# Gate and up products of a hybrid encoder layer by seven block products in place of eight

## The chip, the cores and the metric

The kernel runs on one core of a Trainium2 chip. The metric is the device time of one execution in microseconds; lower is better. The kernel before was timed three times: 723.5, 723.86 and 723.93 us, median 723.86 us.

## The reference, cut to what matters

One layer of an encoder trunk over 512 tokens with 1024 features, all in float32: latent attention and a gated linear recurrence side by side, an output projection, a gated feed-forward part and a per-layer embedding gate. The change lies in the feed-forward part, whose inner width D_FF is 2816, that is 22 tiles of 128 columns.

```
a = mla(c_q, c_kv, k_r, ...)
r = hgrn2(hq, hf_f, hf_b, hi, hg, ...)
x = x + concatenate([a, r]) @ w_o
h = rms_norm(x, g_ffn)
x = x + (silu(h @ w_gate) * (h @ w_up)) @ w_down
gate = sigmoid(rms_norm(x, g_ple) @ w_ple_gate)
x = x + gate * (p @ w_ple_proj)
```

## The kernel before, in words

Activations lie with features on partitions: x is eight tiles `xT[k]` of 128 features by 512 tokens. TensorE multiplies in float32r, so every operand is split into a high part (ScalarE copies it to float32r) and a low part (VectorE subtracts the high part from the operand); `split` does this. A product is then three matmuls, high by high, high by low and low by high (`mm3`, lines 137 to 139), all added up in one PSUM bank. Weights come by DMA from the SyncE queue in chunks of 128 by up to 1024 (`weights`, line 143): a `raw` tile from a pool of four, a `whi` and a `wlo` tile from pools of WB = 3 each. All other tiles of 128 by 512 come from 74 slots that the program hands out itself (`Slots`), the one that has been free longest first; PSUM's eight banks are handed out in the same way.

Up to about 300 us two streams run side by side, the input projections with the recurrence and the attention. Then the second half of the output projection (`w_o_half(1, ...)`) makes the last sums of x, four tiles at a time: k outside, the four output tiles inside. `residual` adds each to x, scales it with the norm's gains and splits it (`hh`, `hl`, lines 133 and 134), and adds its squares for the norm. The factor 1/rms by token (`token_rstd`) isn't multiplied into h: it is put on the products when they leave PSUM (`bc2`).

The feed-forward part (line 947 on) goes through the 22 tiles of the inner width in three parts of 8, 7 and 7 (FPARTS). For each tile f it loads the chunk of `w_gate` and then that of `w_up` (128 by 1024: eight k blocks of 128), multiplies each with all eight feature tiles (eight k, 24 matmuls of 512 columns into a bank `ff`), multiplies with `bc2` on the way out (line 957), applies Silu to the gate, multiplies both (line 962) and splits the result (`ah`, `al`). At the end of a part come the down products: for each of eight output tiles m one chunk of `w_down` and nf x 3 matmuls into a bank `dn`, added to x by `residual`. After the three parts follow the gate of the per-layer embeddings (`pg`) and the output.

The program is written in order and without semaphores. A planner in the tile framework lays out the order of the instructions on each engine: it runs through the program with a cost for each instruction, and each engine takes what is ready, first in program order. So an instruction can be drawn forward past one that isn't ready by the planner's reckoning. On the chip each engine keeps the order laid out and waits where something isn't there. A tile from a pool is given to the instruction that writes it first, once all users of an earlier one have been through.

Of the kernel before, what the change touches and what calls it, by code (L numbers as in the profile page):

```python
# [8 lines left out]
F32 = mybir.dt.float32  # L9
# [6 lines left out]
P = 128  # L16
S = 512
# [5 lines left out]
FPARTS = (8, 7, 7)  # L23
SLOTS = 74
# shares of the two streams
L_TOTAL, D_TOTAL = 97, 135
AHEAD = 2
WB = 3
# [8 lines left out]
# columns of the packed per-partition vectors  # L37
V_MIX, V_FFN, V_PLE, V_QA, V_KVA, V_QN, V_KN, V_LB, V_HGO = 0, 8, 16, 24, 26, 28, 29, 30, 46
NV = 50
# columns of the packed rows (the same for every partition)  # L40
R_QN, R_KN = 0, 64
NR = 128
# columns of the constants that depend on shapes alone
# [11 lines left out]
class Slots:  # L55
    """Tiles of one size, handed out by hand: the one that has been free longest comes next."""
# [19 lines left out]
    def part(self, prefix, n):  # L76
        """Slots of their own from the free ones."""
        s = Slots(self.pool, 0, self.prefix)
        s.free.extend(self.free.popleft() for _ in range(n))
        s.count = 1000 * ord(prefix)  # L80
        return s
# [7 lines left out]
def merge(streams):  # L89
    """Runs generators side by side, by the shares of their totals that they have yielded. One that  # L90
    yields a condition waits until it holds."""
# [16 lines left out]
def v3(t, a, b=None):  # L108
    """A tile's 512 columns as (a, b)."""
    return t.rearrange("p (a b) -> p a b", a=a)  # L110
# [3 lines left out]
def layer_kernel(ctx: ExitStack, tc: tile.TileContext, io, out):  # L114
# [11 lines left out]
    # ---------------------------------------------------------------- helpers  # L126
    def split(hi, lo, src, scale=None, eng=dve):
        """src (times a scale per partition) = hi + lo, each exact in float32r."""
# [14 lines left out]
    def weights(src, cols, lo_eng=None):  # L143
        """A chunk of weights [128, cols]: its parts hi and lo."""
# [13 lines left out]

    def rsqrt_mean(o, ss, n):
        """o = (ss / n + eps) ** -0.5, for a few columns."""  # L160
        w = ss.shape[-1]
        v = small.tile([P, 8], F32, tag="rs_v", name="rs_v")
        dve.tensor_scalar(v[:, :w], ss, 1.0 / n, EPS, ALU.mult, ALU.add)  # L163
        pool.tensor_tensor(o, v[:, :w], mhalf[:, :w], ALU.pow)  # L164

    def token_rstd(sq, keep=None):
        """From sums of squares [128 of the features, tokens]: 1/rms by token, tokens on
        partitions [128, 4] and on columns, the same on every partition [128, 512]."""
# [6 lines left out]
        # the diagonal matrices of 1 / rms, summed over the partitions  # L175
# [13 lines left out]
    def squares(acc, src, first):  # L189
        """acc += src ** 2"""  # L190
# [8 lines left out]
    # ---------------------------------------------------------------- inputs  # L199
# [11 lines left out]
    # loads the activation engine's table while the first inputs are under way  # L211
    act.activation(small.tile([P, 1], F32, tag="first", name="first"), mhalf[:, :1], AF.Exp)

    # ---------------------------------------------------------------- input projection, latents
    # the query's latents, features on partitions
    hT = [(A.get(f"hh{k}", F32R), A.get(f"hl{k}", F32R)) for k in range(KT)]
    cq = [B.get(f"cq{m}") for m in range(2)]
    # the tensor engine's clock rises while it is busy
# [31 lines left out]
    # those of key and value and the rotary key, tokens on partitions  # L250
# [23 lines left out]
    # ---------------------------------------------------------------- rotary tables  # L274
# [17 lines left out]
    # cos(r) = sin(pi / 2 - |r|)  # L292
# [9 lines left out]
    def rope(eng, o, x, c, s, t1, t2):  # L302
        """o = x * [cos, cos] + [x2, x1] * [-sin, sin], all [128, a, 64]"""
# [5 lines left out]
    # ---------------------------------------------------------------- lower bounds of the gates  # L309
# [14 lines left out]
    # ================================================================ latent attention  # L324
# [4 lines left out]
    def attention():  # L329
        """Emits the attention in pieces; yields the tensor engine's time for each."""  # L330
        # 1 / rms of the latents, with the one of the input
        sc = cpool.tile([P, 2 * NT], F32, name="sc")  # by token: query, key and value
# [28 lines left out]
        # the shared rotary key, with its gains, turned  # L361
# [8 lines left out]
        def wsmall(name, cols):  # L370
            """A small matrix of two chunks, two halves each."""
# [11 lines left out]
        # keys and values; per head, tokens on partitions: [128, tile, 128]  # L383
# [3 lines left out]
        rt = [A.get(f"rk{j}") for j in range(NT)]  # rotary parts by tile: [128, (key, query) x head, 64]  # L387
# [67 lines left out]
        def features(tok, g):  # L455
            """[128 tokens, tile, 128] to [128 features, tokens], times gains: hi and lo."""
# [9 lines left out]
        def rotary(pr):  # L466
            """Of two heads: the key's parts (hi, hi) and (lo, lo), the query's (hi, lo)."""
# [78 lines left out]
    # ================================================================ HGRN2  # L546
    # 1 at every step but a chunk's first, for the sums along the chunks
# [7 lines left out]
    # chunks of weights for the dense stream, one ahead of its use  # L555
# [11 lines left out]
    def w_in_tile(d):  # L567
        """One tile of 128 of the input projection's columns: [128 columns, tokens]"""
# [11 lines left out]
    def w_in_tokens(evacuate):  # L580
        """512 columns of the input projection, tokens on partitions, 256 at a time."""
# [16 lines left out]
    def gates(heads):  # L598
        """q, and for each direction k and the sums of log f along the chunks."""
# [10 lines left out]
        # one table of the activation engine after the other  # L610
# [13 lines left out]
        for (h, d), f in zs.items():  # L624
            # log f = log max(f, c) + log min(f / c, 1)
# [17 lines left out]
    def together(emit):  # L643
        """The first, whose operand comes last, and the others right behind it."""
# [5 lines left out]
    def output_gates():  # L650
        """Features on partitions, with the gains of the output norm."""
# [19 lines left out]
    def decays(h):  # L671
        """Of one head, both directions: queries and keys with the decays that go with them."""
        yield lambda: ("gates", h) in done
        for d in range(2):
# [7 lines left out]
            # exponentials of the sums: to the chunk's middle, from there to its end, to its end  # L682
# [17 lines left out]
            # the same for tiles of two chunks  # L700
# [16 lines left out]
    def within(h):  # L717
        """What reaches a step from its own tile of two chunks, as weights [128 s, tile, 128 t]."""
        pd = BL.get("pd")  # within chunks: [128 (chunk, s), direction, tile, 64 t]
        pd4 = pd.rearrange("p (d j t) -> p d j t", d=2, j=NT)  # L720
        px = BL.get("px")  # from a tile's earlier chunk to its later one
# [27 lines left out]
    def carried(h):  # L749
        """The states before the tiles, both directions."""  # L750
# [50 lines left out]
    def finish(h):  # L801
        """Norm, gate and layout of one head's outputs."""
# [27 lines left out]
    def w_o_half(half, src, banks):  # L830
        """x += (src as rows of features) @ half of the output projection's rows"""
        for c in range(2):
            ws = [wnext() for _ in range(2)] if half else None
            os_ = []
            for m in range(4 * c, 4 * c + 4):
# [12 lines left out]
            if half:  # L848
# [4 lines left out]
                for i in range(4):  # L853
                    residual(4 * c + i, os_[i], V_FFN, sq2, h2)
                banks.put(*os_)

# [62 lines left out]
    wlist.extend((io["w_or"][c], 1024) for c in range(4))  # L919
# [4 lines left out]
    def residual(m, o, g, sqacc, hs):  # L924
        """x[m] += o; its squares and its parts hi and lo, with the next norm's gains."""
        dve.tensor_tensor(xT[m], xT[m], o, ALU.add)  # L926
        if g is not None:
            hl = (A.get("hh", F32R), A.get("hl", F32R))
            split(hl[0], hl[1], xT[m], vec[:, g + m : g + m + 1])
            hs.append(hl)  # L930
            squares(sqacc, xT[m], m == 0)

    B = BD.join(BL)
    sq2 = A.get("sq2")
    h2 = []
# [7 lines left out]
    # ---------------------------------------------------------------- feed-forward  # L943
# [3 lines left out]
    for part, nf in enumerate(FPARTS):  # L947
        acts = []
        for f in range(f0, f0 + nf):
            zz = []  # L950
            for name in ("w_gate", "w_up"):
                w = weights(io[name][f], 1024)
                o = B.get("ff")
                for k in range(KT):
# [124 lines left out]
```

## Time and profile before

| what | number |
|---|---|
| runs | 723.5, 723.86, 723.93 us |
| span of the profiled execution | 721.8 us |
| TensorE (matmul) busy | 703.6 us, 97% |
| VectorE busy | 439.3 us, 61% |
| ScalarE busy | 309.2 us, 43% |
| GpSimd busy | 135.8 us, 19% |
| read from memory | 63.68 MB |

The profiled execution has only its span (first to last instruction); the timed runs lie 1.7 to 2.1 us above it, for what comes before and after. Line numbers (L137) are those of the kernel before. Names are those of the program without their numbers: `ff<-hh,whi` is a matmul into a gate or up bank from a feature tile and a weight tile. A matmul's listed duration runs from its start to its result, and neighbours overlap.

### The profile page before, as it was taken

The numbers are of one execution on the slowest core, as the hardware profiler recorded it, in microseconds if no ns is written. First come the engines' busy times: TensorE is split into PE (matmuls) and PEld (weight loads), VectorE is DVE, ScalarE is ACT, GpSimd is POOL, SyncE is SP. The second block draws the span as 40 slices with busy tenths as digits, with TensorE's granted clock in tenths as the row PEclk, the third lists the DMA queues.
The fourth block names the chain that finished last, engine by engine and source line by source line (L and its number), as shares of the span: only waits on it lengthen the run. The fifth ranks groups of instructions, "written<-read, shape, count | busy, mean of one in ns | idle before, by whom it ended". The sixth has DMA issues, their size and how long they took to land.

```text
span 721.8 us, 9167 instructions
## 1 busy us (share of the span) xinstructions
PE 703.6 (97%) x3516; PEld 588.5 (82%) x3516; DVE 439.3 (61%) x733; ACT 309.2 (43%) x573; POOL 135.8 (19%) x126
## 2 busy tenths in 40 slices
PE   8999997998999999999999999999999999999997
PEld 6888885897878888788888888888888888888886
DVE  8954469988999984386545334435433444456573
ACT  5566785576554635355233222223222223244341
POOL 7983577010543511001000000000000000000000
PEclk9999999999999999999999999999999999999999
DMA  8432112111034221033232322232233232233211
GB/s 282 167 114 93 59 36 81 59 30 60 15 103 156 60 78 59 30 118 116 96 109 87 104 101 87 91 114 77 79 108 117 90 108 87 78 105 116 89 59 58
DMA packets 22075, 66.36 MB, mean 92 GB/s; under 512 B 2704, under 2 KB 3984, under 8 KB 22032
## 3 DMA queue, kind: packets, MB, share of 16 engines
q1 hardware_dynamic: 22032, 65.79, 28.0%
q8 instruction: 27, 0.44, 0.2%
q14 instruction: 16, 0.13, 0.1%
HBM read 63.68 MB, written 2.10 MB: 91 GB/s over the span
## 4 chain that ended last, share of the span: by engine, by line
PE 85%; DVE 8%; ACT 3%; DMA 2%; issue 1%; SPq 1%; POOL 0%; ACTq 0%; POOLq 0%
PE ff L137 11%; PE ff L138 11%; PE ff L139 11%; PE dn L138 6%; PE dn L137 6%; PE dn L139 6%; PE wi L139 3%; PE wi L137 3%; PE wi L138 3%; PE pg L139 2%; PE pg L138 2%; PE pg L137 2%; PE wo L137 2%; PE wo L139 2%; PE wo L138 2%; PE po L787 1%
## 5 line engine op out<-in xcount | busy, mean ns | idle before, releaser
L130 ACT ACTIVATE whi<-raw 128x1024 fp32r<-128x1024 f32 (+4 forms) x114 | 116.2, 1019 | 286.6 <-issue 103.1
L131 DVE TENSOR_TENSOR wlo<-raw,whi 128x1024 fp32r<-128x1024 f32 (+4 forms) x108 | 133.7, 1240 | 26.1 <-ACT whi L130 24.8
L137 PE MATMUL ff<-hh,whi 128*128 128x512 f32 x352 | 137.0, 390 | 0.1
L138 PE MATMUL ff<-hl,whi 128*128 128x512 f32 x352 | 136.8, 389 | 0.0
L139 PE MATMUL ff<-hh,wlo 128*128 128x512 f32 x352 | 136.8, 389 | 0.0
L957 DVE TENSOR_TENSOR z<-ff,rsbc 128x512 f32<-128x512 f32 x44 | 30.1, 691 | 109.8 <-PE ff L139 109.2
L164 POOL TENSOR_TENSOR rs_tok<-rs_v,mhalf 128x4 f32<-128x4 f32 x3 | 4.7, 1568 | 391.7 <-DVE rs_v L163 391.7
L137 PEld LDWEIGHTS ff<-hh,whi 128*128 128x128 f32 x352 | 66.1, 188 | 14.3 <-ACT whi L130 0.5
L138 PEld LDWEIGHTS ff<-hl,whi 128*128 128x128 f32 x352 | 66.1, 188 | 13.7
L139 PEld LDWEIGHTS ff<-hh,wlo 128*128 128x128 f32 x352 | 66.1, 188 | 13.6
L137 PE MATMUL dn<-ah,whi 128*128 128x512 f32 x176 | 68.5, 389 | 0.0
L138 PE MATMUL dn<-al,whi 128*128 128x512 f32 x176 | 68.5, 389 | 0.0
L139 PE MATMUL dn<-ah,wlo 128*128 128x512 f32 x176 | 68.5, 389 | 0.0
L139 PE MATMUL wi<-hh,wlo 128*128 128x512 f32 x128 | 51.7, 404 | 3.6 <-DVE wlo L131 3.6
L926 DVE TENSOR_TENSOR x<-x,dn 128x512 f32<-128x512 f32 x24 | 16.5, 687 | 60.5 <-PE dn L139 60.5
L138 PE MATMUL wi<-hl,whi 128*128 128x512 f32 x128 | 51.4, 401 | 0.0
L137 PE MATMUL wi<-hh,whi 128*128 128x512 f32 x128 | 51.0, 400 | 0.0
L137 PEld LDWEIGHTS dn<-ah,whi 128*128 128x128 f32 x176 | 33.0, 188 | 6.9
L139 PEld LDWEIGHTS dn<-ah,wlo 128*128 128x128 f32 x176 | 33.0, 188 | 6.8
L138 PEld LDWEIGHTS dn<-al,whi 128*128 128x128 f32 x176 | 33.0, 188 | 6.8
L139 PEld LDWEIGHTS wi<-hh,wlo 128*128 128x128 f32 x128 | 24.5, 191 | 8.9 <-DVE wlo L131 4.0
L138 PEld LDWEIGHTS wi<-hl,whi 128*128 128x128 f32 x128 | 24.4, 191 | 4.9
(287 smaller groups left out, 1361.9 us busy)
## 6 DMA issues: line engine op xcount, KB each, us to landing
raw<-in_w_gate SPq DMA_DIRECT2D x22, 512.0 KB, 3.3
raw<-in_w_up SPq DMA_DIRECT2D x22, 512.0 KB, 3.2
raw<-in_w_hf SPq DMA_DIRECT2D x16, 512.0 KB, 3.7
raw<-in_w_d SPq DMA_DIRECT2D x16, 448.0 KB, 3.2
x<-in_xT SPq DMA_DIRECT2D x16, 256.0 KB, 5.2
raw<-in_w_d SPq DMA_DIRECT2D x8, 512.0 KB, 3.3
raw<-in_w_pg SPq DMA_DIRECT2D x8, 512.0 KB, 3.2
raw<-in_w_i SPq DMA_DIRECT2D x4, 512.0 KB, 3.4
```

The lines of the kernel that those rows point to most:

```text
L130: act.activation(hi, src, AF.Copy)
L131: eng.tensor_tensor(lo, src, hi, ALU.subtract)
L137: pe.matmul(o, lhsT=l[0], rhs=r[0], start=start, stop=False)
L138: pe.matmul(o, lhsT=l[0], rhs=r[1], start=False, stop=False)
L139: pe.matmul(o, lhsT=l[1], rhs=r[0], start=False, stop=stop)
L164: pool.tensor_tensor(o, v[:, :w], mhalf[:, :w], ALU.pow)
L787: pe.matmul(po[:, ts(j)], lhsT=l, rhs=r, start=n == 0, stop=n == len(terms) - 1)
L926: dve.tensor_tensor(xT[m], xT[m], o, ALU.add)
L957: dve.tensor_tensor(z, o, bc2, ALU.mult)
```

## The change

Two weight tiles f and f + 1 (256 columns of the inner width) are multiplied together. The rows are cut in k 0 to 3 and k 4 to 7, so each matrix is two by two blocks: A11 and A12 are the chunk of f, A21 and A22 that of f + 1; the features are cut in the same two halves of k and in two halves of 256 tokens, B11, B12, B21, B22. The product of two by two blocks takes seven block products instead of eight, by the scheme with sums S1 to S4 of weight blocks, T1 to T4 of feature blocks, and sums of the results. A block product is four k by three matmuls of 256 columns.

`weight_blocks` loads both chunks and makes the four sums of weights on GpSimd, 128 by 512 each; `feature_blocks` makes those of the features on GpSimd once, 128 by 256 each, and `split_blocks` splits them. `products` runs the seven products in three PSUM banks and the sums of results on VectorE. The last sum, S4, of gate and up shares one tile for both (`last_sums`). WB goes from 3 to 4, the pool `sums` has three tiles, the slots go from 74 to 68, and FPARTS from (8, 7, 7) to (8, 8, 6), for even parts; the second half of the output projection makes the x tiles in pairs k and k + 4.

```diff
-FPARTS = (8, 7, 7)
-SLOTS = 74
+FPARTS = (8, 8, 6)
+SLOTS = 68
-WB = 3
+WB = 4
+HS = S // 2
...
+    def weight_blocks(src1, src2, u, last):
+        nw[0] += 1
+        r1 = wpool.tile([P, 1024], F32, tag="raw", bufs=RAWB, name=f"raw{nw[0]}a")
+        r2 = wpool.tile([P, 1024], F32, tag="raw", bufs=RAWB, name=f"raw{nw[0]}b")
+        u1 = wpool.tile([P, 1024], F32, tag="sums", bufs=3, name=f"sums{nw[0]}")
+        sp.dma_start(r1, src1)
+        sp.dma_start(r2, src2)
+        a11, a12, a21, a22 = r1[:, :512], r1[:, 512:], r2[:, :512], r2[:, 512:]
+        s1, s2 = u1[:, :512], u1[:, 512:]
+        t, thi, tlo = u
+        s4 = slice(last * 512, last * 512 + 512)
+        pool.tensor_tensor(s1, a21, a22, ALU.add)
+        pool.tensor_tensor(a21, a11, a21, ALU.subtract)
+        pool.tensor_tensor(s2, s1, a11, ALU.subtract)
+        pool.tensor_tensor(t[:, s4], a12, s2, ALU.subtract)
+        out = {}
+        for n, src, names in (("1", r1, ("A11", "A12")), ("2", r2, ("S3", "A22")), ("3", u1, ("S1", "S2"))):
+            hi = wpool.tile([P, 1024], F32R, tag="whi", name=f"whi{nw[0]}{n}")
+            lo = wpool.tile([P, 1024], F32R, tag="wlo", name=f"wlo{nw[0]}{n}")
+            split(hi, lo, src)
+            for i, name in enumerate(names):
+                out[name] = cut((hi, lo), i * 512, i * 512 + 512)
+        split(thi[:, s4], tlo[:, s4], t[:, s4])
+        out["S4"] = thi[:, s4], tlo[:, s4]
+        return out
+    def last_sums():
+        nw[0] += 1
+        return (wpool.tile([P, 1024], F32, tag="sums", bufs=3, name=f"sums{nw[0]}"),
+                wpool.tile([P, 1024], F32R, tag="whi", name=f"whi{nw[0]}"),
+                wpool.tile([P, 1024], F32R, tag="wlo", name=f"wlo{nw[0]}"))
+    def feature_blocks(z1, z2, t3):
+        c = A.get("t24")
+        pool.tensor_tensor(t3, z2[:, HS:], z1[:, HS:], ALU.subtract)
+        pool.tensor_tensor(z1[:, HS:], z1[:, HS:], z1[:, :HS], ALU.subtract)
+        pool.tensor_tensor(c[:, :HS], z2[:, HS:], z1[:, HS:], ALU.subtract)
+        pool.tensor_tensor(c[:, HS:], z2[:, :HS], c[:, :HS], ALU.subtract)
+        return c
+    def split_blocks(blocks, z1, z2, c):
+        for src, names in ((z1, ("B11", "T1")), (z2, ("B21", "B22")), (c, ("T2", "T4"))):
+            hl = (A.get("bh", F32R), A.get("bl", F32R))
+            split(*hl, src)
+            A.put(src)
+            blocks["tiles"].append(hl)
+            for i, name in enumerate(names):
+                blocks[name].append(cut(hl, i * HS, i * HS + HS))
+    def products(w, b, bank):
+        n = len(b["B11"])
+        def product(o, left, right, start):
+            for k in range(n):
+                l, r = cut(w[left], k * P, k * P + P), b[right][k]
+                kw = dict(skip_group_check=not start)
+                pe.matmul(o, lhsT=l[0], rhs=r[0], start=start and k == 0, stop=False, **kw)
+                pe.matmul(o, lhsT=l[0], rhs=r[1], start=False, stop=False, **kw)
+                pe.matmul(o, lhsT=l[1], rhs=r[0], start=False, stop=k == n - 1, **kw)
+        o1, o2, o3 = (bank.get(f"st{i}") for i in range(3))
+        product(o1[:, :HS], "S2", "T2", True)
+        product(o1[:, HS:], "A11", "B11", True)
+        product(o2[:, :HS], "S3", "T3", True)
+        qc = A.get("qc")
+        act.copy(qc[:, HS:], o1[:, HS:])
+        dve.tensor_tensor(qc[:, :HS], o1[:, :HS], qc[:, HS:], ALU.add)
+        product(o3[:, :HS], "S1", "T1", True)
+        dve.tensor_tensor(qc[:, HS:], o2[:, :HS], qc[:, :HS], ALU.add)
+        product(o1[:, HS:], "A12", "B21", False)
+        z1, z2 = A.get("z1"), A.get("z2")
+        dve.tensor_tensor(z2[:, HS:], o3[:, :HS], qc[:, HS:], ALU.add)
+        product(o2[:, :HS], "A22", "T4", False)
+        product(o3[:, :HS], "S4", "B22", False)
+        return z1, z2, qc, (o1, o2, o3)
...
+            ms = (2 * c, 2 * c + 1, 2 * c + 4, 2 * c + 5) if half else range(4 * c, 4 * c + 4)
+            for m in ms:
                 if not half and m % 2 == 0:
                     w = wnext()
                 o = banks.get("wo")
@@ -850,9 +942,10 @@
                     for i in range(4):
                         a = ((i % 2) * 4 + k) * P
                         mm3(os_[i], cut(ws[i // 2], a, a + P), src[k], k == 0, k == 3)
-                for i in range(4):
-                    residual(4 * c + i, os_[i], V_FFN, sq2, h2)
+                for i in (0, 2, 1, 3):
+                    residual(ms[i], os_[i], V_FFN, sq2, h2)
                 banks.put(*os_)
+                ffn_blocks(c)
...
-    wlist.extend((io["w_or"][c], 1024) for c in range(4))
+    wlist.extend((io["w_or"][c], 1024) for c in (0, 2, 1, 3))
...
-            hl = (A.get("hh", F32R), A.get("hl", F32R))
-            split(hl[0], hl[1], xT[m], vec[:, g + m : g + m + 1])
-            hs.append(hl)
+            if g == V_FFN:
+                hs[m] = A.get("xg")
+                act.activation(hs[m], xT[m], AF.Copy, scale=vec[:, g + m : g + m + 1])
+            else:
+                hl = (A.get("hh", F32R), A.get("hl", F32R))
+                split(hl[0], hl[1], xT[m], vec[:, g + m : g + m + 1])
+                hs.append(hl)
             squares(sqacc, xT[m], m == 0)
+    hb = {n: [] for n in ("B11", "B21", "B22", "T1", "T2", "T3", "T4", "tiles")}
+    def ffn_blocks(c):
+        d = A.get("t3")
+        for i in range(2):
+            k = 2 * c + i
+            z1, z2 = h2[k], h2[k + 4]
+            split_blocks(hb, z1, z2, feature_blocks(z1, z2, d[:, i * HS : i * HS + HS]))
+        hl = (A.get("bh", F32R), A.get("bl", F32R))
+        split(*hl, d)
+        A.put(d)
+        hb["tiles"].append(hl)
+        hb["T3"].extend(cut(hl, i * HS, i * HS + HS) for i in range(2))
...
-        for f in range(f0, f0 + nf):
+        for f in range(f0, f0 + nf, 2):
+            u = last_sums()
             zz = []
-            for name in ("w_gate", "w_up"):
-                w = weights(io[name][f], 1024)
-                o = B.get("ff")
-                for k in range(KT):
-                    mm3(o, cut(w, k * P, k * P + P), h2[k], k == 0, k == KT - 1)
-                z = A.get("z")
-                dve.tensor_tensor(z, o, bc2, ALU.mult)
-                B.put(o)
+            for e, name in enumerate(("w_gate", "w_up")):
+                w = weight_blocks(io[name][f], io[name][f + 1], u, e)
+                z1, z2, qc, o = products(w, hb, B)
+                dve.tensor_tensor(z1[:, :HS], o[0][:, HS:], bc2[:, :HS], ALU.mult)
+                dve.tensor_tensor(z2[:, :HS], o[1][:, :HS], qc[:, :HS], ALU.add)
+                dve.tensor_tensor(z2, z2, bc2, ALU.mult)
+                dve.tensor_tensor(z1[:, HS:], o[2][:, :HS], qc[:, :HS], ALU.add)
+                dve.tensor_tensor(z1[:, HS:], z1[:, HS:], bc2[:, HS:], ALU.mult)
+                B.put(*o)
+                A.put(qc)
                 if name == "w_gate":
-                    act.activation(z, z, AF.Silu)
-                zz.append(z)
-            dve.tensor_tensor(zz[0], zz[0], zz[1], ALU.mult)
-            hl = (A.get("ah", F32R), A.get("al", F32R))
-            split(hl[0], hl[1], zz[0])
-            A.put(*zz)
-            acts.append(hl)
+                    for z in (z2, z1):
+                        act.activation(z, z, AF.Silu)
+                zz.append((z1, z2))
+            for i in range(2):
+                z = zz[0][i]
+                dve.tensor_tensor(z, z, zz[1][i], ALU.mult)
+                hl = (A.get("ah", F32R), A.get("al", F32R))
+                split(hl[0], hl[1], z)
+                A.put(z, zz[1][i])
+                acts.append(hl)
         if part == len(FPARTS) - 1:
-            for hl in h2:
+            for hl in hb["tiles"]:
                 A.put(*hl)
             A.put(bc2)
```

## Rows read from the trace of the kernel before

**Rows 1.** The page: busy time of engines, and the chain that ended last
```profile
span 721.8 us, 9167 instructions
...
PE 703.6 (97%) x3516; PEld 588.5 (82%) x3516; DVE 439.3 (61%) x733; ACT 309.2 (43%) x573; POOL 135.8 (19%) x126
...
PE 85%; DVE 8%; ACT 3%; DMA 2%; issue 1%; SPq 1%; POOL 0%; ACTq 0%; POOLq 0%
```

**Rows 2.** Busy time by stretch, clock, DMA share (x: instructions)
```profile
core 0: us, PE busy (x) PEld busy (x) DVE busy (x) ACT busy (x) POOL busy (x), PEclk, DMA share, GB/s
...
40.00:280.00 240.00, 231.18 (x1369) 195.04 (x1368) 190.33 (x414) 146.70 (x351) 95.52 (x88) 0.99 0.22 71
...
306.60:400.00 93.40, 93.37 (x415) 77.41 (x416) 54.44 (x76) 36.55 (x49) 1.93 (x1) 1.00 0.32 107
```

**Rows 3.** Waits: who waited for whom: us in total, times, longest
```profile
DVE z L957 <- PE ff L139: 109.2, 39, 3.5
...
PE wi L139 <- DVE wlo L131: 3.6, 1, 3.6
```

**Rows 4.** Timeline of TensorE, 512 columns (start, us, engine, line)
```profile
365.12 0.39 PE L137 MATMUL ff<-hh,whi 128*128 128x512 f32 x1
...
367.84 0.39 PE L137 MATMUL ff<-hh,whi 128*128 128x512 f32 x1
```

**Rows 5.** Timeline of TensorE, 256 columns
```profile
714.91 0.28 PE L137 MATMUL pg<-hh,whi 128*128 128x256 f32 x1
...
716.71 0.28 PE L137 MATMUL pg<-hh,whi 128*128 128x256 f32 x1
```

**Rows 6.** Groups of instructions by line: busy us, mean ns | idle before
```profile
L137 PE MATMUL ff<-hh,whi 128*128 128x512 f32 x352 | 137.0, 390 | 0.1
```

**Rows 7.** Timeline of VectorE in the feed-forward part
```profile
357.28 0.69 DVE L962 TENSOR_TENSOR z<-z,z 128x512 f32<-128x512 f32 x1
357.89 1.22 DVE L131 TENSOR_TENSOR wlo<-raw,whi 128x1024 fp32r<-128x1024 f32 x1
359.02 0.69 DVE L131 TENSOR_TENSOR al<-z,ah 128x512 fp32r<-128x512 f32 x1
```

**Rows 8.** Timeline of VectorE at the end, 256 columns
```profile
717.27 0.42 DVE L996 TENSOR_TENSOR z<-pg,rsbc 128x256 f32<-128x256 f32 x1 [1.08 <-PE pg L139]
...
718.63 0.42 DVE L1000 TENSOR_TENSOR z<-z,x 128x256 f32<-128x256 f32 x1
```

**Rows 9.** Timeline of ScalarE in the feed-forward part
```profile
358.01 0.63 ACT L130 ACTIVATE ah<-z 128x512 fp32r<-128x512 f32 x1 [0.64 <-DVE z L962]
361.75 1.06 ACT L130 ACTIVATE whi<-raw 128x1024 fp32r<-128x1024 f32 x1 [3.11 <-PE ff L138]
```

**Rows 10.** Timeline of GpSimd
```profile
94.97 0.74 POOL L307 TENSOR_TENSOR rk<-rt 128x256 f32<-128x256 f32 x1
...
99.86 1.30 POOL L621 TENSOR_TENSOR z<-z,sig 128x512 f32<-128x512 f32 x1 [0.67 <-ACT sig L613]
...
113.45 1.45 POOL L634 TENSOR_TENSOR z<-z,t 128x512 f32<-128x512 f32 x1
114.87 1.71 POOL L307 TENSOR_TENSOR rk<-rt 128x256 f32<-128x256 f32 x1
116.54 3.45 POOL L634 TENSOR_TENSOR z<-z,t 128x512 f32<-128x512 f32 x2
```

**Rows 11.** Timeline of VectorE beside it
```profile
113.70 2.29 DVE L131 TENSOR_TENSOR wlo<-raw,whi 128x1024 fp32r<-128x1024 f32 x1
...
117.58 0.66 DVE L576 TENSOR_TENSOR z<-wi,rsbc 128x512 f32<-128x512 f32 x1
```

**Rows 12.** Timeline of TensorE at the entry to the feed-forward part
```profile
311.33 0.39 PE L139 MATMUL wo<-rTh,wlo 128*128 128x512 f32 x1
311.56 0.39 PE L138 MATMUL ff<-hl,whi 128*128 128x512 f32 x1
```

**Rows 13.** Timeline of ScalarE there
```profile
315.37 0.73 ACT L133 ACTIVATE hh<-x,vec 128x512 fp32r<-128x512 f32 x1
```

More of the change, by code (lines that the diff above doesn't have):

```diff
@@ L834, in w_o_half @@
             os_ = []
-            for m in range(4 * c, 4 * c + 4):
+            ms = (2 * c, 2 * c + 1, 2 * c + 4, 2 * c + 5) if half else range(4 * c, 4 * c + 4)
+            for m in ms:
                 if not half and m % 2 == 0:
@@ L927, in residual @@
         if g is not None:
-            hl = (A.get("hh", F32R), A.get("hl", F32R))
-            split(hl[0], hl[1], xT[m], vec[:, g + m : g + m + 1])
-            hs.append(hl)
-            squares(sqacc, xT[m], m == 0)
+            if g == V_FFN:
[5 more added lines that the diff above has]
+                hs.append(hl)
+            squares(sqacc, xT[m], m == 0)
+    hb = {n: [] for n in ("B11", "B21", "B22", "T1", "T2", "T3", "T4", "tiles")}
[10 more added lines that the diff above has]
+        hb["T3"].extend(cut(hl, i * HS, i * HS + HS) for i in range(2))
     B = BD.join(BL)
     sq2 = A.get("sq2")
-    h2 = []
+    h2 = {}
     for _ in w_o_half(1, rT, B):
```

## The prediction, made before the change was run

> **What bounds the kernel now.** I read the page first [rows 1]: TensorE is busy 97% of the span, VectorE 61%, GpSimd 19%, and the chain that ended last lies on TensorE for 85%. The table of stages [rows 2] says where the change acts. In its first 93.4 us the feed-forward part has TensorE busy for 93.37 at full clock (2.4 GHz), VectorE for 54.44 (58%), GpSimd for 1.93. The list of waits [rows 3] agrees: VectorE waits 109.2 us in all for the matmuls `ff`, while these stand idle for 0.1 us before 352 of them [rows 6]. So a microsecond less of matmul is a microsecond less of time here, as long as the other engines keep up.
>
> Busy time and mean durations don't price a matmul, since they overlap. The starts do. Twelve matmuls of 512 columns start in 367.84 - 365.12 = 2.72 us, 0.2267 us each though each is listed with 0.39 [rows 4]. Fifteen of 256 columns start in 716.71 - 714.91 = 1.80 us, 0.1200 us each [rows 5]. The difference, 0.1067 us for 256 columns, is one column per cycle at 2.4 GHz; a fixed 13.3 ns is left on each matmul, whatever its width.
>
> **The change, part by part.**
>
> *Matmuls.* Removed: 3 x 352 = 1056 matmuls `ff` of 512 columns (three such lines as that of [rows 6]), 1056 x 0.2267 = 239.4 us, that is 10.88 us for one pair of weight tiles (48 matmuls, 22 such pairs). Added: 22 x 7 products x 4 k x 3 parts = 1848 of 256 columns, 1848 x 0.1200 = 221.8 us, 10.08 us a pair, 1.44 us a product. The balance is -17.6 us: an eighth of the columns (28.2 us) less 792 more fixed costs (10.6 us). The Trainium skill (TensorE: Matmul & The Clock Gate, "Back-to-back issue gap") gives a warm gap of N/2.4 + 2.5 ns, thus 215.8 and 109.2 ns; by it the balance would be -26.1 us. The rows show 13.3 ns where it has 2.5, and the measurement decides.
>
> *Work beside the matmuls, for one pair (10.08 us of TensorE).* A VectorE operation starts 0.61 us after one of 512 columns and 1.13 us after one of 1024 [rows 7]; one of 256 is listed with 0.42, from PSUM or SBUF [rows 8], so 0.34 when the next follows directly (0.08 overlaps, as with 512: 0.69 against 0.61). VectorE then has: low parts of three 1024-column and one 512-column operands, 3 x 1.13 + 0.61 = 4.0 us; seven sums and products of 256 columns, 2.4 us; the product of z2 with 1/rms 0.61; half of the gating and of its low parts 1.2. Sum 8.2 us, where before it had 2 x 1.13 + 2 x 0.61 + 1.2 = 4.7 in 10.88. ScalarE has 3 x 1.06 + 0.63 for the high parts [rows 9], about 0.4 for the copy of A11 B11, 0.6 for half of the two Silu, 0.6 for `ah`: 5.4 us, no bound. The loads are the same 44 of 512 KB. GpSimd gets four sums of 512 columns from two SBUF operands; one took 1.30 us by itself [rows 10], so 5.2 us.
>
> *The collision.* These GpSimd sums are not free for VectorE. In [rows 11] a low part of 1024 columns beside a 1.45 us GpSimd sum took 2.29 us, not 1.22: 1.07 us more. And a GpSimd sum of 256 columns behind it took 1.71, not 0.74 [rows 10]. But a VectorE operation fed from PSUM (`z<-wi`) took its usual 0.66 us in the middle of two GpSimd sums. So what reads two SBUF operands excludes GpSimd and is excluded by it. Of the 8.2 us, 6.2 read two SBUF operands (4.0, the two products with 1/rms 0.95, the 1.2), so the two engines' shared time is 6.2 + 4 x 1.07 = 10.5 us a pair, already over TensorE's 10.08. If each sum delays VectorE, that engine alone needs 8.2 + 4.3 = 12.5 us. The Trainium skill (SBUF — State Buffer, "SBUF: two separate sides") calls the shared port pair an exclusive lock, held for the whole instruction; by that rule a sum costs its whole 1.30 us and the shared time is 6.2 + 5.2 = 11.4 us.
>
> *Buffers.* The pools for high and low parts have four tiles each, and a pair needs three of its own and one that gate and up share. So nothing is double-buffered. By the order of the products, S1|S2 is released after product 4, A11|A12 after 5, S3|A22 after 6. The next pair's operands are split in the order A1, A2, S1|S2, so S1|S2, which its first product wants, gets its tile only after product 6. From there ScalarE takes 1.06 us and VectorE 1.22 us, with hand-overs of 0.04 us each (357.28 + 0.69 to 358.01, [rows 7, 9]), 2.4 us in all, against product 7 (1.44 us) and the two matmuls that need only the high part (0.24 us). TensorE waits about 0.8 us: 10.9 us a pair, what a pair takes now, if VectorE is free at that moment. With one GpSimd sum in the way it is 10.9 + 1.07 = 12.0, with two 13.0. The planner may draw other products forward (S3 T3 has a bank of its own), which brings it nearer 10.1.
>
> I take 12.0 us a pair: the round of buffers with one collision, and just below VectorE's 12.5 with all four, since some of the sums will fall beside PSUM-fed work. Bounds: 10.08 (everything covered) and 13.2. The first pair of each of the three parts is prepared during the down products, which keep their 528 matmuls and leave VectorE time. That leaves 19 waits of 1.92: 221.8 + 36.5 = 258.3 us against 239.4, **+18.9 us**.
>
> *Entry to the feed-forward part.* Now the last matmul `wo` starts at 311.33 and `ff` follows at once with the feature tiles that are ready [rows 12]; the last scaled tile comes from ScalarE at 316.1 [rows 13]. After the change a feature pair is usable only when GpSimd has done four dependent sums of 256 columns (4 x 0.74 = 3.0 us [rows 10]), and the two last pairs follow each other on it: from about 315 to 321, then ScalarE's split 0.6 and VectorE's 0.6. Every product runs over all four k, so TensorE has only k = 0 and 1 of products 1, 3 and 4 (18 x 0.12 = 2.2 us) and part of k = 2 to fill 311.6 to 321. I take 6 us of idle time, bounds 0 and 10. The low parts that VectorE saves here (8 x 0.66) are taken back by its 13 new splits.
>
> *Costed at nothing.* 68 slots in place of 74: reuse comes sooner before 300 us, where TensorE idles 8.8 of 240 us [rows 2]; 0 to +4. The fourth weight buffer there: 0 to -3, since one wait for a low part (3.6 us) stands there [rows 3]. New cuts of the down weights, and order of w_or: 0, same bytes and matmuls. Gating of the last pair of a part: two tiles late in place of one, some 4 us behind the matmuls, under the 4.1 us of down matmuls (18 x 0.2267, six earlier tiles) that are ready even so in the first tile, or 2.7 us for the last part with four; 0, at most +2 each.
>
> *Sum.* 721.8 us (span) + 18.9 + 6 = 746.7. The runs' median is 723.86, 2.1 us above the span, which lies around it: **749 us**.
>
> **The rivals.**
>
> A, matmuls decide: the planner's order covers the round of buffers, at most one or two sums delay VectorE, a pair takes 10.1 to 10.5 us. For it: TensorE waits for nobody now, and 8.2 us of VectorE fit 10.08. Against it: [rows 11]. With 10.3: 221.8 + 19 x 0.2 = 225.6, -13.8 + 6, 716 us (706 without the idle entry).
>
> B, the round of buffers decides without collisions, 10.9 us a pair: 221.8 + 19 x 0.82 = 237.4, -2.0 + 6, 728 us; without the entry 722. For it: the sums can run early, as the raw tiles for the next pair are loaded ahead. Against: they run while the low parts run.
>
> C, slower than I forecast: the low part of S1|S2 stands behind two sums and behind the evacuations in VectorE's queue, from 13.2 us a pair: 221.8 + 19 x 3.1 = 280.7, +41.3 + 6, 771 us. For it: a wrong guess of the planner on one engine holds all in strict order. It decides once VectorE's queue at the release of product 6 holds over 2.2 us of work.
>
> **How the numbers follow.** Forecast 0.47 (11.3 to 13.0 us a pair, so 735 to 768), A 0.18, B 0.17, C 0.18. Within 0.2% (1.4 us, about what a measurement of this kernel can tell) are parts of A and B: 0.04. Faster: A and a little of B, 0.20. Slower 0.76. The range leaves out the better half of A and the far end of C: 715 to 775.
>
> **What would show it.** Right: `o` matmuls of 256 columns that start 0.120 us apart within a product, 1848 of them; low parts of 1024 columns at about 2.3 us beside GpSimd, with a mean well over 1.3; TensorE idle once a pair for some 2 us, ended by VectorE's or ScalarE's split; a hole of some us between `wo` and the first products; TensorE under 93% busy. The forecast is wrong if TensorE stays at 97%, or if the low parts stay at 1.22 us beside GpSimd, or if the first products are held up by PSUM evacuation rather than by the splits.

## The result, and the profile after

The changed kernel takes 779.84 us (median of 4 runs, 778.5 to 783.74) against 723.68 for the kernel before beside it: ratio 1.0785, 95% interval 1.0759 to 1.0811. It is slower, as forecast, but 30.8 us beyond the 749 us predicted and outside the range of 715 to 775. The profiled executions' spans are 777.4 and 721.8 us, so 55.6 us are to be found.

The page answers to [rows 1]. TensorE's share fell to 91%, VectorE's rose to 72%, GpSimd's from 19% to 36%, and the chain that ended last lost 14 points on TensorE and gained 10 on VectorE and 4 on GpSimd:

```profile
span 777.4 us, 11197 instructions
...
PE 711.2 (91%) x4308; PEld 629.0 (81%) x4308; DVE 561.3 (72%) x915; ACT 361.4 (46%) x653; POOL 281.4 (36%) x230
...
PE 71%; DVE 18%; POOL 4%; ACT 3%; issue 2%; DMA 1%; SPq 0%; ACTq 0%; DVEq 0%
```

The table of stretches, as in [rows 2], separates the places. Its rows are the first part (from 40 us, up to 248, where its waits lie), the entry to the feed-forward part, and the first and second run of eight pairs (a pair is the two tiles of one matrix, as in the prediction):

```profile
core 0: us, PE busy (x) PEld busy (x) DVE busy (x) ACT busy (x) POOL busy (x), PEclk, DMA share, GB/s
40.00:248.30 208.30, 189.50 (x1040) 158.90 (x1039) 150.97 (x332) 123.84 (x293) 81.43 (x78) 0.96 0.19 61
324.96:361.60 36.64, 16.60 (x58) 13.23 (x58) 34.48 (x40) 19.73 (x34) 26.94 (x21) 0.53 0.09 29
361.60:447.40 85.80, 79.96 (x626) 78.03 (x626) 69.97 (x102) 39.76 (x52) 29.44 (x20) 0.96 0.27 89
490.97:583.15 92.18, 85.46 (x673) 83.83 (x672) 74.82 (x106) 40.92 (x54) 32.09 (x22) 0.96 0.26 83
```

*First part, +13.2 us.* The last matmul `wo` starts at 324.57, not at 311.33 [rows 12]. From 40 us on TensorE has 18.8 us without work where it had 8.8 in a longer stretch, and its granted clock there is 0.96 of full where it was 0.99.

*Entry, +29.9 us.* From the end of `wo` to the steady flow of products 36.6 us pass, in which only 46 product matmuls and the few small ones for the norm's factor (6.7 us at full clock) are done. The kernel before had no gap [rows 12]. TensorE's timeline shows a long wait, one matmul of a first product, a second long wait, and then starts 0.21 us apart instead of 0.12; from 358.6 to 361.3 us the granted clock is 0.50 of full, its lower level (1.2 GHz):

```profile
324.57 0.39 PE L140 MATMUL wo<-rTh,wlo 128*128 128x512 f32 x1
336.72 0.58 PE L229 MATMUL st<-bh,whi 128*128 128x256 f32 x1 [11.76 <-ACT bh L131]
343.09 1.87 PE L261 MATMUL ss<-ones,sq 128*128 128x1 f32 x8 [5.79 <-DVE sq L286]
...
359.04 0.41 PE L231 MATMUL st<-bh,wlo 128*128 128x256 f32 x1
359.25 0.41 PE L229 MATMUL st<-bh,whi 128*128 128x256 f32 x1
```

Meanwhile VectorE, and GpSimd beside it:

```profile
321.82 2.48 DVE L1019 TENSOR_TENSOR x<-x,wo 128x512 f32<-128x512 f32 x4 [4.29 <-PE wo L140]
...
325.36 2.48 DVE L1019 TENSOR_TENSOR x<-x,wo 128x512 f32<-128x512 f32 x4
...
339.03 1.21 DVE L132 TENSOR_TENSOR bl<-xg,bh 128x512 fp32r<-128x512 f32 x1
...
350.84 0.68 DVE L132 TENSOR_TENSOR bl<-t,bh 128x512 fp32r<-128x512 f32 x1
```

```profile
332.31 1.18 POOL L207 TENSOR_TENSOR t<-xg,xg 128x256 f32<-128x256 f32 x1
333.44 1.17 POOL L206 TENSOR_TENSOR xg<-xg 128x256 f32<-128x256 f32 x1
...
342.45 1.71 POOL L182 TENSOR_TENSOR sums<-sums,raw43a 128x512 f32<-128x512 f32 x1
```

All eight updates of x come after 321.8, the last four after the last `wo`. A low part of 512 columns takes 1.21 us beside a GpSimd sum and 0.68 where none runs; a feature sum takes 1.17, not the 0.74 of [rows 10].

In the kernel before, VectorE's updates of x began 8 us before the last `wo`, the gate's first matmul came while `wo` was still running, and the last updates and squares ran beside `ff`:

```profile
303.20 2.48 DVE L926 TENSOR_TENSOR x<-x,wo 128x512 f32<-128x512 f32 x4 [4.97 <-PE wo L139]
...
319.65 2.93 DVE L196 TENSOR_TENSOR sq<-sq,sq 128x512 f32<-128x512 f32 x4
```

```profile
306.63 0.50 PE L137 MATMUL ff<-hh,whi 128*128 128x512 f32 x1
```

*Pairs, +12.5 us.* The three runs of pairs take 85.8, 92.2 and 68.5 us; with 5.5 us of products inside the entry that is 252.0 us against 239.4, 12.6 more (the total above, 55.6, leaves 12.5). A full pair takes 11.5 us, where the prediction had 12.0 and TensorE alone 10.08. The waits (who for whom, us in total, times, longest) name what ends them:

```profile
PE st L229 <- DVE qc L239: 14.7, 5, 4.2
PE st L231 <- DVE wlo L132: 2.8, 3, 1.7
```

`qc` is the evacuation of the first sum of products from PSUM, and not a split. The timelines of VectorE, GpSimd and TensorE around one such wait:

```profile
515.23 1.51 DVE L1071 TENSOR_TENSOR z<-z,rsbc 128x256 f32<-128x256 f32 x1
516.67 3.43 DVE L1080 TENSOR_TENSOR z<-z,z 128x512 f32<-128x512 f32 x2
520.02 0.41 DVE L239 TENSOR_TENSOR qc<-st,qc 128x256 f32<-128x256 f32 x1
```

```profile
515.13 1.33 POOL L180 TENSOR_TENSOR sums<-raw66b 128x512 f32<-128x512 f32 x1 [4.50 <-DMA raw66b<-in_w_gate]
516.54 1.34 POOL L181 TENSOR_TENSOR raw66b<-raw66a,raw66b 128x512 f32<-128x512 f32 x1
517.83 1.71 POOL L182 TENSOR_TENSOR sums<-sums,raw66a 128x512 f32<-128x512 f32 x1
519.62 1.61 POOL L183 TENSOR_TENSOR sums<-raw66a,sums 128x512 f32<-128x512 f32 x1
```

```profile
520.48 0.38 PE L229 MATMUL st<-bh,whi 128*128 128x256 f32 x1 [3.17 <-DVE qc L239]
520.71 0.28 PE L230 MATMUL st<-bl,whi 128*128 128x256 f32 x1
...
523.19 0.41 PE L230 MATMUL st<-bl,whi 128*128 128x256 f32 x1
523.41 0.41 PE L231 MATMUL st<-bh,wlo 128*128 128x256 f32 x1
```

Beside GpSimd's sums the two gating products take 3.43 us (one took 0.69 in [rows 7]) and a 256-column product 1.51 instead of the 0.42 of [rows 8]. `qc` stands behind them in VectorE's queue, and TensorE waits 3.17 us for its bank. A few matmuls later some 15 run at half clock, 1.6 us more. This happens in four of the 22 pairs: at 406, 517, 542 and 655 us two gating products are stretched to 3.4 us, and a wait of 3.2 to 4.2 us follows each time. Where no sum runs beside them the products take 1.28 us, and no wait for `qc` follows:

```profile
566.99 1.28 DVE L1080 TENSOR_TENSOR z<-z,z 128x512 f32<-128x512 f32 x2
568.20 0.41 DVE L239 TENSOR_TENSOR qc<-st,qc 128x256 f32<-128x256 f32 x1
```

Over the three runs of pairs TensorE is idle for 17.7 us and loses some 8.5 to the lower clock (0.96, 0.96 and 0.98 of full): 26 of the 30 us above the floor of 221.8.

### The profile page after: what moved, and what is told of

Its sections match the earlier page's. It is cut to its first block, busy times and chain, and to the rows that moved or that the text cites. A ratio compares the mean times of both kernels' runs of the same rounds, so it can differ in the third digit from the quotient of the medians.

```text
span 777.4 us, 11197 instructions
## 1 busy us (share of the span) xinstructions
PE 711.2 (91%) x4308; PEld 629.0 (81%) x4308; DVE 561.3 (72%) x915; ACT 361.4 (46%) x653; POOL 281.4 (36%) x230
## 4 chain that ended last, share of the span: by engine, by line
PE 71%; DVE 18%; POOL 4%; ACT 3%; issue 2%; DMA 1%; SPq 0%; ACTq 0%; DVEq 0%
PE st L229 7%; PE st L231 7%; PE st L230 7%; PE dn L140 5%; PE dn L138 5%; PE dn L139 5%; DVE wlo L132 5%; PE wi L139 3%; PE wi L138 3%; PE wi L140 3%; PE pg L140 2%; PE pg L139 2%; PE pg L138 2%; PE wo L138 2%; DVE z L1080 2%
## 5 line engine op out<-in xcount | busy, mean ns | idle before, releaser
L229 PE MATMUL st<-bh,whi 128*128 128x256 f32 x616 | 178.9, 294 | 26.4 <-DVE qc L239 14.7
L230 PE MATMUL st<-bl,whi 128*128 128x256 f32 x616 | 179.0, 293 | 2.5 <-DVE bl L132 2.3
L231 PE MATMUL st<-bh,wlo 128*128 128x256 f32 x616 | 175.4, 293 | 3.0 <-DVE wlo L132 2.8
L229 PEld LDWEIGHTS st<-bh,whi 128*128 128x128 f32 x616 | 123.2, 201 | 28.9 <-DVE qc L239 15.7
L230 PEld LDWEIGHTS st<-bl,whi 128*128 128x128 f32 x616 | 123.3, 200 | 4.9 <-DVE bl L132 4.7
L231 PEld LDWEIGHTS st<-bh,wlo 128*128 128x128 f32 x616 | 121.2, 200 | 5.4 <-DVE wlo L132 5.3
L131 ACT ACTIVATE whi<-raw 128x1024 fp32r<-128x1024 f32 (+4 forms) x70 | 69.4, 993 | 76.0 <-PE dn L139 33.2
L132 DVE TENSOR_TENSOR wlo<-raw,whi 128x1024 fp32r<-128x1024 f32 (+4 forms) x64 | 79.8, 1250 | 20.6 <-ACT whi L131 20.4
L131 ACT ACTIVATE whi<-sums 128x1024 fp32r<-128x1024 f32 (+1 forms) x44 | 36.1, 842 | 32.4 <-PE st L230 13.2
L132 DVE TENSOR_TENSOR wlo<-sums,whi 128x1024 fp32r<-128x1024 f32 (+1 forms) x44 | 44.5, 1032 | 1.5 <-ACT whi L131 1.4
```

The lines of the kernel that those rows point to most:

```text
L131: act.activation(hi, src, AF.Copy)
L132: eng.tensor_tensor(lo, src, hi, ALU.subtract)
L229: pe.matmul(o, lhsT=l[0], rhs=r[0], start=start and k == 0, stop=False, **kw)
L230: pe.matmul(o, lhsT=l[0], rhs=r[1], start=False, stop=False, **kw)
L231: pe.matmul(o, lhsT=l[1], rhs=r[0], start=False, stop=k == n - 1, **kw)
```

## The experiments

Each is compared with runs of the kernel before on the same chip (723.8 to 724.4 us).

**1, 2: first part.** Fewer slots alone, and more weight buffers alone, in the kernel before.

```
-SLOTS = 74          -WB = 3
+SLOTS = 68          +WB = 4
```

> The kernel before with 68 slots in place of 74 and nothing else. In the changed kernel the last matmul of the output projection starts 13.2 us later than before (324.57 against 311.33 us), ahead of everything that the block products touch. Theory 'slots': tiles are reused sooner, so instructions of the attention and recurrence wait for the last user of a slot; then this kernel loses most of it, 8 to 14 us, about 732 to 738 us, and its last wo starts at 319 to 325 us. Rival 'weight buffers': the fourth buffer changes the order in which weights are split; then this stays within 2 us of 723.7. Rival 'order': neither alone matters, the planner's order moved with the text behind; also within 2 us.

> The kernel before with four buffers for high and low parts of weights in place of three (74 slots kept). Theory 'slots': no loss, 721 to 725 us. Rival 'weight buffers': 8 to 14 us slower, about 732 to 738 us. Rival 'order': within 2 us of 723.7, as with 68 slots.

Measured: 68 slots 741.18 us, ratio 1.0219 (1.0192 to 1.0246), last `wo` at 328.9; four weight buffers 725.63, ratio 1.0018 (1.0007 to 1.0029). So the slots alone cost 17 us, more than the theory's 8 to 14; the buffers cost next to nothing. In the kernel with 68 slots TensorE has waits before 325 us that the list of the kernel before does not have (its longest there is the 3.6 us of [rows 3]):

```profile
PE s L137 <- ACT qkh L133: 4.2, 1, 4.2
PE wi L137 <- DVE z L576: 3.9, 1, 3.9
PE ropeT L472 <- POOL rk L307: 3.6, 2, 3.4
```

The changed kernel has two of them again:

```profile
PE ropeT L562 <- POOL rk L397: 6.6, 2, 3.5
PE s L138 <- ACT qkh L134: 4.7, 2, 4.2
```

Whether the slots act through tiles that come free late or through another order that the planner lays out isn't shown.

**3, 4, 5: pairs.** The weight sums left out; the same sums on VectorE; S1|S2 split first.

```
-        pool.tensor_tensor(s1, a21, a22, ALU.add)     (and the other three)
3:       (none; S1|S2 and S4 taken from the raw tiles)
4: +     dve.tensor_tensor(s1, a21, a22, ALU.add)      (and the other three)
5: -     for n, src, names in (("1", ...), ("2", ...), ("3", ...)):
   +     for n, src, names in (("3", ...), ("1", ...), ("2", ...)):
```

> The changed kernel without the four GpSimd sums of weights for each pair of tiles: S1, S2 and S4 are taken from the raw chunks, S3 from A21, so the numbers are not those of the layer, but every split, matmul, load and evacuation is there. Theory 'collision': the sums stretch the VectorE operations with two SBUF operands (two gating products take 3.43 us instead of 1.3), the sum qc waits behind these, TensorE waits 3.2 us for it once in two pairs and then runs at half clock. Without the sums a pair comes to 10.1 to 10.4 us instead of 11.5, minus 24 to 30 us in the 22 pairs, and some more at the entry: 744 to 754 us. Rival 'buffers': the round of four weight buffers holds TensorE whatever GpSimd does; then a pair stays at 10.9 us or more and the kernel at 762 us or above.

> The changed kernel with the four sums of weights for each pair of tiles on VectorE, each 0.61 us without GpSimd beside it. Theory 'collision': VectorE then has 8.2 + 2.4 = 10.6 us a pair and nothing that stretches it, TensorE 10.08; a pair takes 10.6 to 11.0 us instead of 11.4, minus 9 to 18 us: 761 to 771 us. Rival 'work': VectorE was short of time by its own work and GpSimd relieved it; then 2.4 us more on it makes a pair 12 us or longer and the kernel slower than 785 us.

> The changed kernel with S1|S2 split first of the three operands of a pair (it gets the buffer that is released first) instead of last. Theory 'collision': nothing but the order of the splits changes and the gating products are stretched as before; within 5 us of 779.8. Rival 'buffers': the release of the third buffer after product 6 costs TensorE 0.8 us or more a pair; then 14 to 25 us faster, 755 to 766 us.

Measured: without the sums 744.33 (ratio 1.0268, 1.0239 to 1.0296); on VectorE 761.18 (1.0507, 1.0468 to 1.0547); other order 778.43 (1.0748, 1.0721 to 1.0775). The second run of eight pairs in kernel 3, and in kernel 10 below, whose sums are all on VectorE:

```profile
475.19:555.82 80.63, 80.63 (x673) 80.63 (x672) 63.46 (x106) 40.45 (x54) 0.00 (x0) 1.00 0.31 101
```

```profile
483.90:569.10 85.20, 82.17 (x674) 81.08 (x673) 76.05 (x127) 40.67 (x54) 0.00 (x0) 1.00 0.28 91
```

Without the sums a pair takes 80.63 / 8 = 10.08 us, TensorE's floor to two digits, with the same round of buffers. So the buffers don't hold the pairs, GpSimd's sums do. With the sums on VectorE, though it gets four more operations a pair, a pair takes 85.20 / 8 = 10.65. So the work was dearer on the engine with room, beside the busier one, than on the busier one itself. The order of the splits changes next to nothing.

**6, 7: entry.** The feature sums on VectorE; the feature sums left out.

```
-        pool.tensor_tensor(t3, z2[:, HS:], z1[:, HS:], ALU.subtract)   (and the other three)
6: +     dve.tensor_tensor(t3, z2[:, HS:], z1[:, HS:], ALU.subtract)    (and the other three)
7:       (none; T1 to T4 taken from the feature tiles)
```

> The changed kernel with the 16 sums of feature blocks (128 by 256) on VectorE instead of GpSimd. In the changed kernel these took GpSimd 1.17 us each, from 328 to 355 us, and TensorE had nearly nothing from 325 to 345 and ran at half clock to 361 us. Theory 'entry on GpSimd': 16 sums of 0.34 us on VectorE and none of the collisions, so the entry falls from 36.6 to 18 to 24 us, 764 to 770 us. Rival 'entry on VectorE': VectorE was busy all through this stretch and only gets more to do; within 4 us of 779.8.

> The changed kernel without the 16 sums of feature blocks: T1 to T4 are taken from the feature tiles themselves, so the numbers are not those of the layer; all 13 splits at the entry and everything behind are there. Theory 'sums': the entry (36.6 us from the last wo to steady products, 6.8 of it products) is the chain of feature sums on GpSimd; without them it falls to 12 to 18 us and the kernel to 755 to 762 us. Rival 'no cover': x, the scaled tiles and 13 splits take VectorE and ScalarE 15 us or more after the last wo anyway, and a block product needs all of them, while the products before could go k by k; then the entry stays at 22 to 30 us and the kernel at 765 to 774 us.

Measured: 773.96 (1.0684, 1.0657 to 1.0711) and 768.31 (1.0606, 1.0586 to 1.0626). Kernel 6 lies between its theory and its rival; kernel 7 is where the rival, missing cover, had it. Even without the feature sums the steady products start 27.7 us after the end of the last `wo` (325.2 to 352.95).

**8: 74 slots in the changed kernel**, with S1, S2 and S4 in slots, for which S1|S2 had to be split in two operations.

```
-SLOTS = 68
+SLOTS = 74
-        u1 = wpool.tile([P, 1024], F32, tag="sums", bufs=3, ...)
+        s1, s2, t = (A.get(n) for n in ("s1", "s2", "s4"))
-                split(hi, lo, src)
+                split(hi[:, :512], lo[:, :512], s1); split(hi[:, 512:], lo[:, 512:], s2)
```

> The changed kernel with 74 slots again; the room comes from the pool of sums, whose three tiles of 1024 columns are taken from the slots instead (S1, S2 and S4 as tiles of 512, so S1|S2 is split in two operations). Theory 'slots': the last wo starts at 311 to 314 us as in the kernel before, and the kernel takes 764 to 770 us. Rival 'order': the 13 us of the first 325 us belong to the planner's order with the block products behind, not to the slots; then wo stays at 320 to 325 us and the kernel within 4 us of 779.8.

Measured: 806.66 (1.1125, 1.1082 to 1.1168), 27 us slower than the change itself, against both theories. The last `wo` did come back to 311.2; but a pair took 13.4 us in the second run of eight. Two edits were mixed here, and the next runs part them.

**9, 10, 11: no sums at all; all sums on VectorE; the same with 74 slots** (as in 8).

> Left out: the sums of the weights and those of the features; the products run on operands of the same shapes taken from the tiles themselves, so the output isn't the layer's. Nothing collides any more. Theory (what is left of the entry is missing cover: x updates, squares, 14 low parts, scaling, all needed before the first product can end): VectorE's list is some 24 us, so 22 us stay between the last wo and the steady products, 11.5 us less than with the feature sums at worst: 733 us (730 to 738). Rival (the sums are the entry, the rest hides as it did before the change): 10 us or less stay between, 744 - 22 = 722 us (719 to 726), below the kernel before.

> All sums, of weights and of features, on VectorE; GpSimd has none left, the computation is whole. Theory (in the entry GpSimd's sums and VectorE's operations stretch each other, 1.17 us a feature sum for 0.74 and 1.21 us a low part for 0.68, on top of missing cover): no stretch is left, VectorE's list from the first x update is 4.9 (x) + 4.6 (weight low parts) + 4.3 (squares) + 8.5 (feature low parts) + 5.4 (feature sums) + 3.0 (weight sums) + 1.9 = 32.6 us from 321.8, so the steady products start near 355 and not 360: 755 us (752 to 758) against the 761 of the kernel with only the weight sums there. Rival (the order of VectorE's queue decides, not the stretch): the sixteen sums come on top of a queue that is full, 761 to 766.

> 74 slots again, the sums' tiles taken from them, and all sums on VectorE; the computation is whole. Theory (the slots cost the first part 13 us and nothing else; the kernel with 74 slots and GpSimd's sums lost in its pairs by stretched sums that held slots): 13 us less than with 68 slots and all sums on VectorE, 742 us (739 to 746). Rival (taking the sums' tiles from the common slots makes each pair wait for the reuse of a slot, whatever engine sums): 12.3 us a pair as with GpSimd, over 760 us.

Measured: 736.32 (1.0164, 1.0148 to 1.0180); 761.68 (1.0506, 1.0476 to 1.0537); 782.34 (1.0791, 1.0768 to 1.0814). In kernel 9, near its theory of 733, no sum is left anywhere, and the entry still has 24.05 us, with VectorE busy for 22.75 of them:

```profile
324.75:348.80 24.05, 15.18 (x59) 12.90 (x59) 22.75 (x42) 19.28 (x35) 1.38 (x1) 0.57 0.13 45
```

In kernel 10 nothing stretches (a feature sum on VectorE takes 0.42 us, a low part 0.69), but the sums stand in a queue that is full: the steady products start at 358.5 against 359.4 in kernel 4. The theory of that run, 755 us, fell; the rival's 761 to 766 held. Kernel 11 was to take 742 us: its last `wo` came at 314.6, but a pair took 13.1 us in the second run. By kernel 11 alone the slots would seem to bring nothing; the last run parts them from the split.

**12: kernel 10 with S1|S2 split in two operations**, nothing else.

```
-            split(hi, lo, src)
+            if n == "3": split(hi[:, :512], lo[:, :512], s1); split(hi[:, 512:], lo[:, 512:], s2)
+            else: split(hi, lo, src)
```

> Only the split of S1|S2 is taken in two operations of 512 columns on each of ScalarE and VectorE, as the kernels with 74 slots had it; 68 slots, the sums in tiles of their own, all sums on VectorE; the computation is whole. Theory (the reuse of common slots by the sums is what the kernels with 74 slots lost): no change but 22 times the fixed part of one more operation beside covered work, 762 us (759 to 767). Rival (two splits in place of one hold ScalarE's queue before the copy of the first product, and TensorE waits 2.4 us a pair for it): 762 + 22 x 1.4 = 792 us, from 780.

Measured: 794.56 (1.0976, 1.0956 to 1.0995), 32.9 us more than kernel 10: 1.5 us a pair on average for one more operation on each of two engines. That is the rival's 792, not the theory's 762. ScalarE's timeline and TensorE's waits (second run of pairs) show how:

```profile
516.61 1.15 ACT L131 ACTIVATE whi<-sums 128x512 fp32r<-128x512 f32 x2 [0.71 <-PE st L234]
520.93 1.06 ACT L131 ACTIVATE whi<-raw64a 128x1024 fp32r<-128x1024 f32 x1 [3.17 <-PE st L234]
521.90 0.62 ACT L131 ACTIVATE ah<-z 128x512 fp32r<-128x512 f32 x1
522.49 0.37 ACT L242 COPY qc<-st 128x256 f32<-128x256 f32 x1
```

```profile
PE st L233 <- DVE qc L243: 12.0, 6, 2.7
```

The next pair's high part, which waits 3.17 us for a buffer, was put ahead of the copy `qc`, which needs no weight buffer, and TensorE waits behind both. Kernels 11 and 12 differ by the slots alone (and where the sums lie): 782.34 against 794.56. So 74 slots are worth 12.2 us in the changed kernel, 9.9 of them by the last `wo` (314.6 against 324.4). What made kernel 8 slow is then most likely the split too; with the sums on GpSimd the split wasn't run alone. Why the order of the queues tips with it was not followed further.

## Why the prediction was wrong

*Failed: "68 slots in place of 74: 0 to +4", taken as nothing.* It cost 13.2 us. The bound came from 8.8 us of idle time of TensorE in that part [rows 2], as if little idle time meant much slack. It says the opposite: TensorE was busy for 96% there, and what came late showed nearly in full. Run 1, and 12 against 11, show 17 and 12 us for the slots.

*Failed: "I take 6 us of idle time, bounds 0 and 10" for the entry.* It was 29.9. The prediction priced what the change adds on GpSimd (dependent sums, with 0.74 us each) and let all else hide as before. Runs 7 and 9 give the parts: of the 36.6 us, 8.9 go with the feature sums (36.6 to 27.7), 3.6 more with the weight sums (27.7 to 24.1). The other 24.1 hold some 7 of work, so some 17 are missing cover, the half clock after the waits among them. VectorE's list of x updates, squares and low parts, 23 us long in kernel 9, ran beside `wo` and `ff` before. Now a block product is only 12 matmuls of 256 columns, each k wants two feature tiles and their sums, and the x updates come together at the end, so hardly any product runs beside the list. That the cover is missing is shown by run 9; how much of it each of these costs wasn't parted, and no other order of VectorE's and ScalarE's queues was tried. The prediction saw that "every product runs over all four k", but counted the list from the last scaled tile of the kernel before [rows 13] instead of from its own first update. The rate was wrong too: the collision it used for the pairs (1.07 us) it didn't use here, where VectorE is just as full.

*Right in its cause, wrong in its path: the pairs.* +12.5 us instead of +18.9, 11.5 us a pair instead of 12.0. The matmul term (10.08 us) is exact, as run 3 shows. That GpSimd's sums and VectorE hold each other up is shown by runs 3 and 4. The Trainium skill (SBUF — State Buffer, "SBUF: two separate sides") has the shared port pair as an exclusive lock. The trace agrees in kind: beside each other a feature sum and a VectorE operation of 512 columns go by turns, one of each in 1.13 us (332.31 to 333.44), where alone they take 0.74 and 0.61 (1.35 together, so the turns aren't shown to exclude each other to the end). Wrong was the place. The prediction hung the collision on the low part of S1|S2 and the round of buffers; run 5 changes that round and moves nothing, run 3 keeps it and reaches the floor. The wait is for `qc` behind stretched gating products, which the prediction had listed as what would prove it wrong. It is also not one of 1.92 us in nearly every pair but one of 3.2 to 4.2 us in four of 22, with half clock after it. So 12.0, a round of buffers that costs nothing (run 3) plus one collision, came near 11.5 in part by luck. The price of a sum was too high as well: the 2.29 us of [rows 11] lie beside two GpSimd sums (one to 114.90, the next from 114.87), not one, and in the second run of pairs VectorE is busy 74.82 us with the sums and 63.46 without, 1.4 us a pair for four sums where the prediction had 4 x 1.07.

The three differences, +13.2, +23.9 and -6.4 us, make up the 30.8 but for rounding.

*Right:* the buffers of the first part as nearly nothing (0.2% slower by run 2, where 0 to -3 us was said), the end (within half a microsecond), the 2.1 us around the span, and the sign. Rival C's 771 us is nearer, but for a reason that did not happen: the pairs take 11.5 us on average, not 13.2.

For the kernel without any sum the terms add up, though the third is taken from its own trace: -17.6 (matmuls) + 13.2 (slots) + 17 (cover) = +12.6, and it measures +11.9 (736.32 - 724.42). The sums cost the other 43 us. On VectorE they cost 25 (761.68 - 736.32). No version here reaches the kernel before: an eighth of the multiplications is worth 17.6 us, and cover and slots alone take more.

## What to carry to other kernels

Before an algorithm with fewer multiplications is priced, list what becomes needed at once: operands that had arrived one k at a time, and were hidden by that, come nearly whole in front of the products. Space is a cost like time: where the bounding engine is 96% busy, as here, fewer buffers upstream can show in full, and one run of the old kernel with the new size gives a first price (17 us here, 12 to 13 in the changed kernel). An idle engine is no free engine if its work and that of the next busiest go by turns, as here: time the pair of them side by side, or do the work on the busier one.

## What was not expected of the hardware

The lower clock came after its cause was over: after a wait of 3.17 us TensorE ran at full rate for twelve matmuls, then at 0.21 us a start for some 15 (521.9 to 525.3, granted clock 0.50), so the price of this wait was its length and half as much again. And one operation of 1024 columns against two of 512, 0.07 us longer on VectorE by their durations (1.29 against 1.22), cost 1.5 us a pair through the order of the queues.
